# Second matrices of the MLPs: seven products over six input tiles instead of four, and two of the weight sums made by adding transfers

## The chip, the cores and the metric

The kernel runs on one core of one Trainium2 chip. The metric is the device time of one execution in microseconds. Engines are named as in the profile: PE (matmul), PEld (its weight load), DVE (vector), ACT (scalar), POOL (GpSimd), SP (issues the transfers); `SPq` and the like are an engine's sequencer. Tensors in SBUF have 128 partitions; PSUM holds banks of 128 x 512 float32.

## The reference, cut to what matters

An encoder trunk of two layers for 256 rows (`T`) of width 2048 (`D`) in float32. Both layers have an attention and a squared-ReLU MLP; the change is in the MLPs:

```python
def sq_relu_mlp(h, g, w1, w2):
    a = jax.nn.relu(rms_norm(h, g) @ w1)
    return (a * a) @ w2

h = h + sq_relu_mlp(h, mlp_norm_g[layer], mlp_w1[layer], mlp_w2[layer])   # 2048 -> 8192 -> 2048
```

All else (the first layer's attention with a forget gate, shared keys and values, the second layer's attention over chunks with a position bias, the output projections) is computed by both kernels in the same way.

## The kernel before, in words

**Products.** Activations are stationary, weights stream: a matmul takes a 128 x 128 block of the transposed activations and 512 columns of a weight tile. For float32 accuracy every operand is split into a high part that PE's fp32r form holds exactly and a low rest, and each product is three passes (`passes`, L408, L410, L412): high by high, low activation by high weight, high activation by low weight. A **unit** is 128 x 1024 of weights: two input tiles (of the 16 that make up 2048) by one **panel** of 512 output columns. With two blocks of 128 rows it has 2 x 2 x 3 = 12 matmuls.

**Feeding.** `units` lists all weights in the order of use. `load` (L164) has SP bring a unit to one of four `raw` buffers; `issue` (L175) has ACT write its high part (L184) and DVE the low one (L185) to three buffers each (`hi`, `lo`); `fetch` (L188) keeps three split units and three loaded ones ahead of PE. `keep_order` (L35) ties the instructions of DVE, ACT, PE and SP to the order in which the program writes them, so each engine works in that order and an instruction that waits holds up what stands behind it.

**Fill.** Side work (attention steps, turning an output through DRAM so that it is the next product's activations, squaring) lies in slots: `run_fill` runs one slot after each unit, `add_fill` appends. A step that has to wait for PE, a transfer or another engine is thus put some units later.

**The MLP.** `mlp` (L769) goes through four chunks of 2048 hidden columns. A chunk has two pairs of panels of the first matrix and two **pairs** of the second one, which adds the chunk's hidden tiles to the output. In each pair, 4 of the 16 input tiles, two rows blocks and the two panels form a 2 x 2 by 2 x 2 block product; with half the input tiles, one row block and one panel per entry it would take eight products. The kernel takes the seven of Strassen's scheme in Winograd's form: "11" and "22" and "21" are weight blocks as they are, T1, T2, T3, T4 are sums of them. Each product is a **form** (`Form`), with two input tiles: 1 x 2 x 3 = 6 matmuls (`form_products`). The sums on the side of the activations (`sums`, L230) are made once per chunk or layer.

`Pair.items` names the work: `f0` to `f6` are the forms in the order 11, T3, T2, T1, 21, T4, 22; `a2` to `a7` and `b2` to `b7` the units of the other 12 input tiles for the two panels. The order of a pair is `f0 rest f1 rest f2 rest f3`, where `rest` is the previous pair's `b5 b6 b7`, and then the string in `head`. Four PSUM banks hold the pair, and forms land in more than one entry: f1's product is copied out by ACT to `P7` (L856), f0's bank copied (L853), and DVE adds the pieces to other banks after f2 (L837) and after `a2` (L845).

**The tiles of a pair.** `prepare` (L762) runs after each unit. `Pair.units` says at how many units before the pair's f0 the tiles 12, 11, 22, 21 are brought (`bring`, L744, transfers by SP to buffers named `k` and `v`, two of each, which the attention uses at other times), and T1 and T3 are made (`make`, L747, a DVE add or subtract at L760). T1 and T3 go to buffers named `bias`, of which there are two, shared with the attention's bias and the scaled input `y` in `split_turned`; the first pair uses the attention's `prob` room. T2 is made over 12 after f0 and T4 over 11 after f1.

**POOL** does a few small things in the attention (an inverse root per head, a mask) and none in the MLP.

Of the kernel before, what the change touches and what calls it, by code (L numbers as in the profile page):

```python
# [15 lines left out]
P = 128  # L16
T = 256
# [14 lines left out]
REL = 384  # L32

# [13 lines left out]
def trunk(ctx: ExitStack, tc: tile.TileContext, xT, xr, gs, hg, bf, wgate, w_in, w_oa, w1a, w2a,  # L47
          w_kv, w_qb, w_ob, w1b, w2b, rel, out):
# [23 lines left out]
    def load_x(i):  # L72
        raw_x[i] = qkv.tile([P, GH, T], F32, name="xin", tag="kv"[i // 2], bufs=2)
        SY.dma_start(raw_x[i], xT[:, i * GH : (i + 1) * GH, :])
# [9 lines left out]
    ones = const.tile([P, T], F32, name="ones")  # L84
    V.memset(ones, 1.0)
    warm = ps_o.tile([P, 512], F32, name="pt", tag="po")
    for _ in range(11):
        TE.matmul(warm[:, :P], ones[:, :P], ones[:, :P], start=True, stop=True)
# [18 lines left out]
    class Form:  # L107

        def __init__(self, pair, i):
            self.pair, self.name = pair, ("11", "T3", "T2", "T1", "21", "T4", "22")[i]  # L110
# [8 lines left out]
    class Pair:  # L119
# [3 lines left out]
        def __init__(self, src, first, order, third):  # L123
            self.src = [[src[first + q * 8 + u] for u in range(8)] for q in range(2)]
            self.third, self.ps, self.t, self.room, self.units = third, None, {}, None, (9, 8, 7, 6, 5, 2)
            self.head = {"early": "a2 f4 a3 f5 b2 f6 b3 a4 b4 a5 a6 a7", "late": "a2 f4 a3 f5 b2 f6 b3 a4 a5 b4 a6 a7",
                         "": "a2 f4 a3 f5 a4 f6 a5 a6 a7 b2 b3 b4"}[order]

        def items(self, names):
            return [(self, "abf".index(i[0]), int(i[1])) for i in names.split()]  # L130

    def plan_mlp(w1, w2, tail):
        n, pairs = w1.shape[0] // NCH, []
        for c in range(NCH):
            for src, late in ((w1, ""), (w2, "late")):
                for q in range(2):
                    pairs.append(Pair(src, c * n + 16 * q, (late if pairs else "early") if q == 0 else "", len(pairs) % 2 == 0))
        pairs[0].units, pairs[1].units, pairs[2].units = (15, 13, 11, 8, 10, 8), (9, 8, 7, 6, 3, 2), (9, 8, 7, 6, 1, 2)
# [6 lines left out]
        units.extend(Form(p, i) if q == 2 else p.src[q][i] for p, q, i in plan)  # L145
        return plan
# [6 lines left out]
    plan_a = plan_mlp(w1a, w2a, tail_a)  # L153
# [5 lines left out]
    plan_b = plan_mlp(w1b, w2b, tail_b)  # L159
# [15 lines left out]
    def issue(parts=1):  # L175
        if not raws:
            load(parts)
        raw, cuts = raws.popleft()
        if not cuts:
            raw, cuts = raw.pair.t[raw.name], [slice(0, UN)]  # L180
        hi = wsp.tile([P, UN], F32R, name="hi")
        lo = wsp.tile([P, UN], F32R, name="lo")
# [3 lines left out]
        ready.append((hi, lo))  # L186

    def fetch(ahead=AHEAD, early=EARLY):  # L188
        while (units or raws) and len(ready) <= ahead:
# [3 lines left out]
        return ready.popleft()  # L193
# [36 lines left out]
    def sums(a, fs):  # L230

        w = [wk.tile([P, 512], F32, name="sum", tag="wk") for _ in range(2)]

        def part(i):
            v = w[i // 2][:, i % 2 * 256 : i % 2 * 256 + 256].rearrange("p (g t) -> p g t", g=2)
# [739 lines left out]
```

## Time and profile before

| | |
|---|---|
| median of 3 runs | 2108.54 us (2107.03, 2108.95, 2108.54) |
| the profiled execution | 2109.01 us, of which its span is 2107.2 us |
| granted TensorE clock | 1.00 of full speed |
| transfers | 491.63 MB, mean 233 GB/s; queue q1 took 71.2% of 16 engines' time |
| instructions | PE 9332, DVE 1812, ACT 1431, POOL 47 |

A page's first part gives each engine's busy time, its share of the span and its count of instructions. A matmul's length in a row is the time from its start to its modelled end, and matmuls overlap, so the pace is read from starts. In rows of groups, `x638 | 775.8, 1219 | 296.3 <-ACT ...` is: count, busy us and mean ns of one, idle us of the engine just before them and what ended it. In windows, "x" is the count in brackets behind the busy us; then come granted clock, DMA share and GB/s. Rows of transfers have the count, the size and the median us from issue to landing. Lines (L408) are those of the kernel before; in parts on the changed kernel they are its own.

### The profile page before, as it was taken

Reading aid. Unit: us, or ns where it says so; the run is one execution under the profiler, and the core shown is the slowest. Engines: PE = TensorE matmul, PEld = TensorE weight load, DVE = VectorE, ACT = ScalarE, POOL = GpSimd, SP = SyncE. Lnnn points to the kernel's source line nnn. Section 1 sums busy time; section 2 is a strip of 40 time slices with the busy share of each in tenths; the row PEclk is TensorE's granted clock in tenths of the full one; section 3 lists DMA queues with packets and bytes.
Section 4 is the critical chain, followed back from the end, with each engine's and each line's share of the span. In section 5 each row is a group of like instructions: output and inputs, shape, how many; then the busy total and the mean of one; then the engine's idle time right before and its main releaser. Section 6 shows DMA issues by size and latency. Waiting matters only on the chain.

```text
span 2107.2 us, 26036 instructions
## 1 busy us (share of the span) xinstructions
PE 2099.1 (100%) x9332; PEld 1741.2 (83%) x9332; DVE 1587.3 (75%) x1812; ACT 1191.4 (57%) x1431; POOL 48.7 (2%) x47
## 2 busy tenths in 40 slices
PE   9999999999999999999999999999999999999999
PEld 8788888888888888888888888888888888888887
DVE  6777676887788777778767677678877877887775
ACT  6545455665466565556575455456654654665653
POOL 1001000000000000000001000000000000000000
PEclk9999999999999999999999999999999999999999
DMA  8787778776676676577678777787766666766774
GB/s 289 236 257 231 234 250 272 241 238 231 216 241 212 211 250 230 188 245 259 194 242 259 238 233 233 227 279 240 257 227 202 232 230 217 236 216 210 244 239 146
DMA packets 182594, 491.63 MB, mean 233 GB/s; under 512 B 36784, under 2 KB 74048, under 8 KB 182464
## 3 DMA queue, kind: packets, MB, share of 16 engines
q1 hardware_dynamic: 182464, 489.96, 71.2%
q8 instruction: 73, 1.20, 0.2%
q14 instruction: 57, 0.47, 0.1%
HBM read 450.01 MB, written 39.87 MB: 232 GB/s over the span
## 4 chain that ended last, share of the span: by engine, by line
PE 99%; DMA 1%; SPq 0%; ACT 0%; DVE 0%; issue 0%; DVEq 0%; ACTq 0%
PE acc L408 26%; PE acc L410 26%; PE acc L412 26%; PE s L408 6%; PE s L412 6%; PE s L410 6%; DMA raw<-in_w_in 1%; PE po L581 1%; PE s L550 1%; PE po L582 0%; PE s L549 0%; PE s L670 0%; DMA turn<-z 0%; SPq L294 0%; ACT hi L184 0%
## 5 line engine op out<-in xcount | busy, mean ns | idle before, releaser
L185 DVE TENSOR_TENSOR lo<-raw,hi 128x1024 fp32r<-128x1024 f32 (+1 forms) x642 | 778.3, 1216 | 296.8 <-ACT hi L184 286.5
L184 ACT ACTIVATE hi<-raw 128x1024 fp32r<-128x1024 f32 (+1 forms) x642 | 677.6, 1057 | 515.2 <-PE acc L410 394.7
L408 PE MATMUL acc<-hi,act 128*128 128x512 f32 x2306 | 632.9, 393 | 2.9 <-ACT hi L184 2.9
L410 PE MATMUL acc<-hi,act 128*128 128x512 f32 x2306 | 623.8, 389 | 0.0
L412 PE MATMUL acc<-lo,act 128*128 128x512 f32 x2306 | 623.5, 389 | 0.0
L410 PEld LDWEIGHTS acc<-hi,act 128*128 128x128 f32 x2306 | 432.8, 188 | 90.4
L412 PEld LDWEIGHTS acc<-lo,act 128*128 128x128 f32 x2306 | 432.8, 188 | 89.9
L408 PEld LDWEIGHTS acc<-hi,act 128*128 128x128 f32 x2306 | 430.8, 188 | 90.9 <-ACT hi L184 3.8
L184 ACT ACTIVATE hi<-w 128x1024 fp32r<-128x1024 f32 x160 | 169.5, 1059 | 153.8 <-PE acc L410 94.4
L185 DVE TENSOR_TENSOR lo<-w,hi 128x1024 fp32r<-128x1024 f32 x160 | 194.8, 1218 | 69.3 <-ACT hi L184 68.3
L408 PE MATMUL s<-hi,act 128*128 128x512 f32 x448 | 121.1, 389 | 0.0
L410 PE MATMUL s<-hi,act 128*128 128x512 f32 x448 | 121.0, 389 | 0.0
L412 PE MATMUL s<-lo,act 128*128 128x512 f32 x448 | 121.0, 389 | 0.0
L184 ACT ACTIVATE hi<-wT 128x1024 fp32r<-128x1024 f32 x60 | 63.6, 1059 | 62.1 <-PE acc L410 41.6
L410 PEld LDWEIGHTS s<-hi,act 128*128 128x128 f32 x448 | 84.1, 188 | 17.5
L412 PEld LDWEIGHTS s<-lo,act 128*128 128x128 f32 x448 | 84.1, 188 | 17.5
L408 PEld LDWEIGHTS s<-hi,act 128*128 128x128 f32 x448 | 84.0, 188 | 17.4
L185 DVE TENSOR_TENSOR lo<-wT,hi 128x1024 fp32r<-128x1024 f32 x60 | 73.2, 1220 | 28.0 <-ACT hi L184 27.8
L760 DVE TENSOR_TENSOR wT<-w,w 128x1024 f32<-128x1024 f32 x60 | 73.1, 1218 | 0.0
L584 ACT ACTIVATE act<-po 128x256 fp32r<-128x256 f32 x32 | 12.3, 385 | 91.1 <-PE po L582 91.1
L492 POOL TENSOR_TENSOR rn<-vv,mhalf 128x4 f32<-128x4 f32 x32 | 43.3, 1366 | 389.9 <-DVE vv L491 389.7
L585 DVE TENSOR_TENSOR act<-po,act 128x256 fp32r<-128x256 f32 x32 | 13.6, 425 | 51.3 <-ACT act L584 51.3
(164 smaller groups left out, 1347.7 us busy)
## 6 DMA issues: line engine op xcount, KB each, us to landing
raw<-in_w_in SPq DMA_DIRECT2D x96, 512.0 KB, 4.5
raw<-in_w1a SPq DMA_DIRECT2D x96, 512.0 KB, 4.3
raw<-in_w2a SPq DMA_DIRECT2D x96, 512.0 KB, 4.4
raw<-in_w1b SPq DMA_DIRECT2D x96, 512.0 KB, 4.3
raw<-in_w2b SPq DMA_DIRECT2D x96, 512.0 KB, 4.3
raw<-in_w_kv SPq DMA_DIRECT2D x64, 512.0 KB, 4.5
turn<-z SPq DMA_DIRECT2D x60, 512.0 KB, 4.2
q<-turn SPq DMA_DIRECT2D x168, 128.0 KB, 3.9
```

What stands on the lines that cost most here:

```text
L184: S.activation(hi[:, c], raw[:, c], AF.Copy)
L185: V.tensor_tensor(lo[:, c], raw[:, c], hi[:, c].bitcast(F32), op=ALU.subtract)
L408: TE.matmul(ps[:, cols], xh, cut(hi, j), start=first, stop=False, **kw)
L410: TE.matmul(ps[:, cols], xl, cut(hi, j), start=False, stop=False, **kw)
L412: TE.matmul(ps[:, cols], xh, cut(lo, j), start=False, stop=last, **kw)
L492: G.tensor_tensor(rn, vv, mhalf, op=ALU.pow)
L550: TE.matmul(s[:, P : 3 * P], q[:, a, P:T], k[:, a], start=True, stop=True)
L581: TE.matmul(po[:, :T], v[:, 0, a * P : (a + 1) * P], pT[:, :2], start=True, stop=False)
L584: S.activation(o[i][:, 0], po[:, :T], AF.Copy)
L585: V.tensor_tensor(o[i][:, 1], po[:, :T], o[i][:, 0].bitcast(F32), op=ALU.subtract)
L760: V.tensor_tensor(t[name], t[a], t[b], op=op)
```

## The change

For the second matrices (`w2`), the seven products now take six input tiles instead of four. Such pairs are called **wide**: a weight block has 128 x 1536 (`WIDE`), and the host lays `w2` out in two arrays, blocks of 1536 columns for the products (`w2f`) and units for the other ten input tiles (`w2s`). Each form consists of `f`, two input tiles and 6 matmuls as before, and a half `h`, the third tile with 128 x 512 and 3 matmuls, which has one split buffer each (`hih`, `loh`). The order in a wide pair is `f0 h0 rest f1 h1 rest f2 h2 rest f3 h3 a3 f4 h4 b3 f5 h5 a4 f6 h6 b4 a5 a6 a7`; the first matrices' pairs keep four input tiles and the order of before.

All signs are turned so that every weight sum is an addition. T2 goes over T3, T1 over 12, T4 over 11 (first matrices) or over T2 (wide). In wide pairs T1 and T4 are transfers that POOL issues (`put`, L801) and that add a block from HBM to what lies in SBUF; T2 is summed as soon as T3 is split and T4 added as soon as T2 is split. f0 and f1 have changed banks: after f1 ACT copies its bank to `P7` (L873) and writes minus f0's bank into it (L874), on which f2 goes on; DVE's first sum has turned signs.

The sums of hidden tiles are made for the third tile too. The units at which tiles are brought and summed, and the slots of the hidden tiles' steps, have other numbers. `bias` has one buffer of 1536 columns instead of two, and small tiles of the first attention lie in it at the start. The core of the diff:

```diff
+WIDE = UN + 512
...
+        def plan(self, rest):
+            made = [self.items(f"f{i} h{i}" if self.wide else f"f{i}") for i in range(7)]
+            own = {"early": "a2 F a3 F b2 F b3 a4 b4 a5 a6 a7", "": "a2 F a3 F a4 F a5 a6 a7 b2 b3 b4",
+                   "wide": "a3 F b3 F a4 F b4 a5 a6 a7"}[self.order].split()
+            plan = made[0] + rest[:1] + made[1] + rest[1:2] + made[2] + rest[2:] + made[3]
+            n = 4
+            for i in own:
+                if i == "F":
+                    plan += made[n]
+                    n += 1
+                else:
+                    plan += self.items(i)
+            return plan, self.items("b5 b6 b7")
...
+            for q in range(2):
+                at = c * n + 16 * q
+                src = [[w1[at + 8 * j + u] for u in range(8)] for j in range(2)]
+                order = "" if pairs else "early"
+                when = (25, 20, 9, 15, 10, 8) if not pairs else (9, 7, 8, 6, 3, 2) if q and not c else (9, 7, 8, 6, 5, 1) if q else (7, 5, 6, 4, 3, 2)
+                pairs.append(Pair({k: src[int(k[1]) - 1][int(k[0]) - 1] for k in names}, src, order, len(pairs) % 2 == 0, when))
+            for q in range(2):
+                at = 2 * c + q
+                src = [[None] * 3 + [w2s[10 * at + 5 * j + u] for u in range(5)] for j in range(2)]
+                when = (7, 5, 6, 4, 3, 2) if q else (9, 7, 8, 6, 5 if c else 3, 1)
+                pairs.append(Pair({k: w2f[4 * at + i] for i, k in enumerate(names)}, src, "wide", len(pairs) % 2 == 0, when))
         plan, rest = [], [(tail, 0, u) for u in range(KT // UA - 3, KT // UA)]
         for p in pairs:
-            f = p.items("f0 f1 f2 f3")
-            plan += [f[0], rest[0], f[1], rest[1], f[2], rest[2], f[3]] + p.items(p.head)
-            rest = p.items("b5 b6 b7")
...
+            form, half = raw, raw.half
+            raw, cuts = form.pair.t[form.name], [slice(0, 512 if half else UN)]
+            if half:
+                raw = raw[:, UN:]
+        n = cuts[-1].stop
+        hi = wsp.tile([P, n], F32R, name="hi" if n == UN else "hih", bufs=3 if n == UN else 1)
+        lo = wsp.tile([P, n], F32R, name="lo" if n == UN else "loh", bufs=3 if n == UN else 1)
         for c in cuts:
             S.activation(hi[:, c], raw[:, c], AF.Copy)
             V.tensor_tensor(lo[:, c], raw[:, c], hi[:, c].bitcast(F32), op=ALU.subtract)
-        ready.append((hi, lo))
+        ready.append((hi, lo, n < UN))
+        if form and half == form.pair.wide:
+            if form.name == "T3":
+                make(form.pair, "T2")
+            elif form.name == "T2" and half:
+                put(form.pair, "T4")
+
+    def half_next():
+        u = raws[0][0] if raws else units[0]
+        return isinstance(u, Form) and u.half
...
-        while (units or raws) and len(ready) <= ahead:
+        while (units or raws) and sum(1 for r in ready if not r[2]) <= ahead and not (half_next() and any(r[2] for r in ready)):
...
-        V.tensor_tensor(part(0), a[1][0], a[1][1], op=ALU.add)
-        V.tensor_tensor(part(1), part(0), a[0][0], op=ALU.subtract)
-        V.tensor_tensor(part(2), a[0][0], a[1][0], op=ALU.subtract)
+        V.tensor_tensor(part(0), a[1][0], a[1][1], op=ALU.subtract)
+        V.tensor_tensor(part(1), a[0][0], part(0), op=ALU.subtract)
+        V.tensor_tensor(part(2), a[1][0], a[0][0], op=ALU.subtract)
         V.tensor_tensor(part(3), a[0][1], part(1), op=ALU.subtract)
...
+    def room(tag, name, dtype=F32):
+        return qkv.tile([P, WIDE], dtype, name=name, tag=tag, bufs=1 if tag == "bias" else 2)
...
+                c = {3: 0, 2: 1, 1: 2, 6: 3}[i]
+                c = c * P if half else c * 256 + g * P
+                xp = [fs[k + 2 * half][:, c : c + P] for k in range(2)]
+            items.append((ps[i not in (4, 5)][i in (0, 5)], xp, g % 2, i < 2 and g == 0, i < 2 and g == stop))
...
     def bring(p, name):
-        t = qkv.tile([P, UN], F32, name="w" + name, tag="kv"[name[1] == "2"], bufs=2)
-        SY.dma_start(t, p.src[int(name[1]) - 1][int(name[0]) - 1])
-        p.t[name] = t
+        p.t[name] = room("kv"[name in ("12", "21")], "w" + name)
+        SY.dma_start(p.t[name][:, : WIDE if p.wide else UN], p.big[name])
 
     def make(p, name):
         t = p.t
-        if name in ("T1", "T3"):
-            if p.room is not None:
-                t[name] = p.room[:, (name == "T3") * UN : (name == "T3") * UN + UN]
-            else:
-                t[name] = qkv.tile([P, GH * REL], F32, name="w" + name, tag="bias", bufs=2)[:, :UN]
-        elif name == "T2":
-            t[name] = t["12"]
+        if name == "T3":
+            t[name] = prob.tile([P, 9 * 3 * P], F32, name="wT3", tag="p", bufs=1) if p.order == "early" else room("bias", "wT3")
         else:
-            t[name] = t["11"]
-        a, b, op = {"T1": ("12", "11", ALU.subtract), "T3": ("22", "12", ALU.subtract),
-                    "T2": ("T3", "11", ALU.add), "T4": ("21", "T2", ALU.subtract)}[name]
-        V.tensor_tensor(t[name], t[a], t[b], op=op)
+            t[name] = t[{"T1": "12", "T2": "T3", "T4": "11"}[name]]
+        a, b = {"T1": ("12", "11"), "T3": ("22", "12"), "T2": ("T3", "11"), "T4": ("21", "T2")}[name]
+        d, a, b = (t[i][:, : WIDE if p.wide else UN] for i in (name, a, b))
+        V.tensor_tensor(d, a, b, op=ALU.add)
+
+    def put(p, name):
+
+        at, other = {"T1": ("12", "11"), "T4": ("T2", "21")}[name]
+        p.t[name] = p.t[at]
+        G.dma_start(p.t[name][:, :WIDE], p.big[other], accum_op=ALU.add)
 
     def prepare(p, d):
-        if d == p.units[0] and p.units[0] > 9:
-            p.room = prob.tile([P, 9 * 3 * P], F32, name="wTT", tag="p", bufs=1)
-        for name, at in zip(("12", "11", "22", "21", "T1", "T3"), p.units):
+        for name, at in zip(("12", "22", "21", "11", "T3", "T1"), p.units):
             if d == at:
-                (make if name[0] == "T" else bring)(p, name)
+                (bring if name[0] != "T" else put if p.wide and name == "T1" else make)(p, name)
...
+            f, kind, k = plan[i - 1]
+            done = k if i and kind > 1 and kind == 2 + f.wide else None
+            if done == 1:
+                f.t["P7"] = wk.tile([P, 512], F32, name="p7", tag="wk")
+                S.activation(f.t["P7"], f.ps[1][0], AF.Copy)
+                S.activation(f.ps[1][0], f.ps[1][1], AF.Copy, scale=-1.0)
+            if q > 1:
+                form_products(p.ps, hi, lo, p.x, p.fs, u, q == 3, 1 + p.wide)
+                if u == 2 and q == 2 + p.wide:
+                    V.scalar_tensor_tensor(p.ps[0][1], p.ps[1][0], -1.0, p.t["P7"], op0=ALU.mult, op1=ALU.subtract)
             else:
                 products(p.ps[q], hi, lo, p.x, u, not units and not ready, p.fast)
+                if p.fast and (q, u) == (0, p.own):
+                    V.tensor_tensor(p.ps[1][1], p.ps[1][0], p.t["P7"], op=ALU.add)
                 run_fill()
                 if u == KT // UA - 1:
                     for b in range(NB):
                         p.evac[q](b, p.ps[q][b])
-                if p.fast and (q, u) == (0, 2):
-                    V.tensor_tensor(p.ps[1][1], p.ps[1][0], p.t["P7"], op=ALU.add)
                 nxt = next((j for j in starts if j > i), None)
                 if nxt is not None:
                     d = sum(1 for it in plan[i:nxt] if it[1] < 2)
                     prepare(plan[nxt][0], d)
-            if i and plan[i - 1][1:] in ((2, 0), (2, 1)):
-                f = plan[i - 1][0]
-                if plan[i - 1][2] == 0:
-                    S.activation(f.ps[0][0], f.ps[1][0], AF.Copy)
-                else:
-                    f.t["P7"] = wk.tile([P, 512], F32, name="p7", tag="wk")
-                    S.activation(f.t["P7"], f.ps[1][1], AF.Copy)
-                    make(f, "T4")
+            if done == 1 and not f.wide:
+                make(f, "T4")
+            elif done == 2:
+                S.activation(f.ps[0][0], f.ps[1][1], AF.Copy)
```

More of the change, by code (lines that the diff above doesn't have):

```diff
@@ L121, in trunk @@
         fast = True
[L123 to L127, printed above, removed]
-        def items(self, names):
-            return [(self, "abf".index(i[0]), int(i[1])) for i in names.split()]
@@ L132, in plan_mlp, with __init__ @@
-    def plan_mlp(w1, w2, tail):
+        def __init__(self, big, src, order, third, units):
+            self.big, self.src, self.third, self.units, self.order = big, src, third, units, order
+            self.ps, self.t, self.wide, self.own = None, {}, order == "wide", 3 if order == "wide" else 2
+        def items(self, names):
+            return [(self, "abfh".index(i[0]), int(i[1])) for i in names.split()]
+        def plan(self, rest):
[11 more added lines that the diff above has]
+            return plan, self.items("b5 b6 b7")
@@ L133, in plan_mlp @@
+    def plan_mlp(w1, w2f, w2s, tail):
         n, pairs = w1.shape[0] // NCH, []
+        names = ("11", "12", "21", "22")
         for c in range(NCH):
[L135 to L138, printed above, removed]
+            for q in range(2):
[9 more added lines that the diff above has]
+                pairs.append(Pair({k: w2f[4 * at + i] for i, k in enumerate(names)}, src, "wide", len(pairs) % 2 == 0, when))
@@ L433, in products, with form_products @@
                 passes(items, hi, lo, c, **kw)
-    def form_products(ps, hi, lo, x, fs, i):
+    def form_products(ps, hi, lo, x, fs, i, half, stop):
         items = []
-        for g in range(2):
+        for g in (2,) if half else range(2):
             if i in (0, 4, 5):
@@ L647, in head_gains @@
         yield
-    wgr = const.tile([P, KT * H], F32, name="wgr")
+    early = room("bias", "early")
+    wgr = early[:, : KT * H]
     ct = {}
@@ L886, in rel_bias @@
     def rel_bias(g, box):
-        rb = qkv.tile([P, GH, REL], F32, name="bias")
+        rb = room("bias", "rb").rearrange("p (a t) -> p a t", a=GH)
         src = bass.AP(tensor=rel.tensor, offset=rel.offset + g * GH * REL, ap=[[1, P], [REL, GH], [1, T]])
@@ L942 @@
     rel = np.zeros((H, REL), np.float32)
+    wide = [_wide(i["mlp_w2"][j]) for j in range(2)]
     rel[:, REL - i["b_rel"].shape[2] :] = i["b_rel"][0]
```

116 lines of the change are left out of this document (58 added, 58 removed).

## The prediction

> **What bounds the kernel now.** I read the page's engine table first, then its chain, then who PE waited for, and last the time lines of one steady pair.
>
> ```profile
> span 2107.2 us, 26036 instructions
> ...
> PE 2099.1 (100%) x9332; PEld 1741.2 (83%) x9332; DVE 1587.3 (75%) x1812; ACT 1191.4 (57%) x1431; POOL 48.7 (2%) x47
> ...
> PE 99%; DMA 1%; SPq 0%; ACT 0%; DVE 0%; issue 0%; DVEq 0%; ACTq 0%
> ...
> PEld acc L408 <- ACT hi L184: 3.8, 3, 2.0
> ...
> PE acc L408 <- ACT hi L184: 2.9, 2, 1.6
> ```
>
> PE is busy for all but 8.1 us of the span, and the chain that ended last is PE from end to end. PE waits for another engine hardly at all: the two wait rows (total, times, longest) are all that there is of it between its first matmul and its last, 3 and 2 times. So time goes away only with matmuls, and every stall that the change makes on PE counts in full. The profiled execution took 2109.01 us, 1.81 us more than its span; the median of the three runs is 2108.54 us, 0.47 us below the profiled one. I sum in differences and put them on the median.
>
> The price of one matmul comes from PE's time line in a second-matrix pair (columns: start, length, engine, line, what, count). The form f1 has three passes of two matmuls, `rest` three passes of four.
>
> ```profile
> 506.62 0.61 PE L410 MATMUL acc<-hi,Sh 128*128 128x512 f32 x2
> 507.07 0.62 PE L412 MATMUL acc<-lo,Sh 128*128 128x512 f32 x2
> 507.52 1.07 PE L408 MATMUL s<-hi,act 128*128 128x512 f32 x4
> 508.43 1.07 PE L410 MATMUL s<-hi,act 128*128 128x512 f32 x4
> 509.34 1.07 PE L412 MATMUL s<-lo,act 128*128 128x512 f32 x4
> 510.24 0.62 PE L408 MATMUL acc<-hi,Sh 128*128 128x512 f32 x2
> 511.60 1.07 PE L408 MATMUL s<-hi,act 128*128 128x512 f32 x4
> ...
> 502.08:544.24 42.16, 42.16 (x187) 34.92 (x186) 32.40 (x31) 21.15 (x22) 0.00 (x0) 1.00 0.59 199
> 628.56:670.72 42.16, 42.16 (x187) 34.92 (x186) 32.47 (x30) 26.64 (x28) 0.00 (x0) 1.00 0.73 243
> ```
>
> A unit of 12 matmuls takes 510.24 - 507.52 = 2.72 us, a form of 6 takes 511.60 - 510.24 = 1.36 us, so one takes 0.2267 us. Two windows follow, each from one pair's f0 to the next pair's: the second and the first pair of a chunk's second matrix (columns: length, busy PE, PEld, DVE, ACT, POOL with counts, clock, DMA share, GB/s). Both are 42.16 us = 186 x 0.2267, with no gap, at full granted clock. DVE has 9.7 us free, ACT more, and the DMA engines are 59% and 73% busy. That is the room the change must live in.
>
> **What goes.** A second-matrix pair had 7 forms of 6 matmuls and 24 units of which 4 are replaced, so 12 x 12 + 42 = 186. With six input tiles it has 7 forms of 6, 7 halves of 3 and 10 units of 12: 63 + 120 = 183. That is 3 per pair, in 16 pairs (2 layers x 4 chunks x 2): 48 matmuls x 0.2267 = **-10.9 us**. The order of the built program agrees: PE has 48 instructions fewer, nothing else of PE changes in number. The first matrices keep their 186.
>
> **What comes on DVE and ACT.** Durations:
>
> ```profile
> L184 ACT ACTIVATE hi<-raw 128x1024 fp32r<-128x1024 f32 x638 | 675.3, 1060 | 514.9 <-PE acc L410 394.7 <-PE s L410 76.7 <-DMA raw<-in_w_in 14.7
> L184 ACT ACTIVATE hi<-raw 128x512 fp32r<-128x512 f32 x4 | 2.3, 620 | 0.3 <-DMA raw<-in_w_in 0.3
> L185 DVE TENSOR_TENSOR lo<-raw,hi 128x1024 fp32r<-128x1024 f32 x638 | 775.8, 1219 | 296.3 <-ACT hi L184 286.0 <-PE acc L410 4.6 <-DMA q<-turn 2.9
> L185 DVE TENSOR_TENSOR lo<-raw,hi 128x512 fp32r<-128x512 f32 x4 | 2.6, 686 | 0.5 <-ACT hi L184 0.5
> L760 DVE TENSOR_TENSOR w<-w,w 128x1024 f32<-128x1024 f32 x32 | 38.9, 1217 | 0.0
> L853 ACT ACTIVATE acc<-s 128x512 f32<-128x512 f32 x16 | 9.3, 582 | 0.0
> L856 ACT ACTIVATE p<-acc 128x512 f32<-128x512 f32 x16 | 9.3, 582 | 0.0
> ```
>
> DVE per pair before: 19 splits x 1.219 + 4 sums x 1.217 = 28.0 us. After: 17 x 1.219 + 7 half splits x 0.686 + 2 sums over 1536 columns. No row has 1536; going on from 512 to 1024 (0.686 to 1.219) gives 1.75 us, between one and two of the 1.217. Sum 29.0 us: +1.0 us in a pair that is 0.7 us shorter, so about 33.4 of 41.5 us. ACT: 17 x 1.060 + 7 x 0.620 + 3 x 0.582 against 19 x 1.060 + 2 x 0.582, +2.8 us. The new sums of hidden tiles (four short DVE adds and one split per chunk) fall in first-matrix pairs, beside PE. All this I cost at nothing, hidden by PE; the cover ends only where one of them is what PE waits for next. There is one such place.
>
> **The new wait in front of f2.** Before, f1's product went to a bank of its own and f2 went on in f0's bank, with only a copy to be made later. Now f1 and f2 share `ps[1][0]`: after f1 and its half h1, ACT must copy the bank out (P7) and overwrite it with minus M1; f2's first matmul waits for the second. ACT's own time line at that place before:
>
> ```profile
> 507.32 1.06 ACT L184 ACTIVATE hi<-raw 128x1024 fp32r<-128x1024 f32 x1 [0.64 <-PE acc L410]
> 508.28 0.58 ACT L856 ACTIVATE p<-acc 128x512 f32<-128x512 f32 x1
> 509.54 1.07 ACT L184 ACTIVATE hi<-wT 128x1024 fp32r<-128x1024 f32 x1 [0.67 <-PE s L410]
> ...
> 84.08 1.06 ACT hi L184
> 85.15 0.04 issue
> 85.19 1.20 PE acc L408 x4
> ```
>
> Two ACT instructions follow each other 0.10 us closer than their lengths (507.32 to 508.28 for one of 1.06), and PE starts 0.05 us after the ACT result it waits for (85.14 to 85.19). In a first-matrix pair the next split starts 0.2 us before `rest` (507.32 against 507.52), P7 ends 1.34 after its start, the negated copy at about 1.98, and PE needs f2 only at 2.72: hidden, by 0.7 us. In a wide pair the half-split of T2 stands ahead of it, and its single buffer is free only when h1's second pass ends, at about the start of `rest` (t = 0; as before, 0.09 us after a pass that ends 0.39 us from its last start). Then: half split 0.03 to 0.65, split of the next unit 0.55 to 1.61, P7 1.51 to 2.09, negated copy, which overwrites what P7 reads and so can't overlap it, 2.14 to 2.72, PE at 2.77 to 2.81 instead of 2.72. I take **0.1 us x 16 = +1.6 us**. This holds if ACT is free at t = 0. Before it come, from the end of h0's second pass 4.7 us earlier: T3's half on ACT 0.62 and on DVE 0.69, T2's sum 1.75, T2's split on ACT 1.06, together 4.1 and the hand-overs: some 0.5 us to spare. Bounds: 0 below; above, a sum of 2 x 1.217 us and a DVE step of 0.69 in front of it eat the 0.5 and give 0.9 us more.
>
> **The adding transfers.** T1 and T4 of wide pairs are no longer DVE sums but transfers issued by POOL that add the other tile from HBM, 768 KB each, 32 in all. The trace has neither an adding transfer nor one by POOL. The nearest rows:
>
> ```profile
> raw<-in_w2a SPq DMA_DIRECT2D x96, 512.0 KB, 4.4
> w<-in_w2a SPq DMA_DIRECT2D x32, 512.0 KB, 5.3
> bias<-cd SPq DMA_DIRECT2D x4, 768.0 KB, 6.7
> ...
> 73.25 10.75 DMA raw<-in_w_in
> ```
>
> Counted with 2.72, 1.36 and 0.68 us from the end of h1: T4's transfer may start when T2's half is split, at about 1.5. PE is at f3 from 7.5, a3 from 9.5, f4 from 12.2, b3 from 14.3, f5 from 17.0; f5's low pass starts at 17.9, and one ACT split and one DVE split (2.4 us with their hand-overs) come before it. So T4 must land by 15.5: **14.0 us**, and until then nothing but ACT waits. Behind the waiting split on ACT stand h5's and a4's; PE needs a4 only at 19.0, so they are not worse off. T1 starts when T3 is summed and has more (some 17 us). POOL has nothing else there (0.00 busy in both windows), so nobody queues behind it. For the cost I take 10 us, nearest to the 6.7 us row and something for the sum's second operand; the ends are 6.7 and, from the 10.75 us that 512 KB took in the crowded start, 1.5 x 10.75 = 16.1 us. At 10 us it costs PE **nothing**. The Trainium skill's page "Collectives: The Full Stack" (section "The bandwidth ceiling: the fold count and why AG ≠ RS ≠ AR") says that an add in a transfer reads two sources, and that those reads, not the arithmetic, halve the rate. By that, an estimate from the row is 2 x 6.7 = 13.4 us: still in time, with 0.6 us left; no run shown here tests it.
>
> The tiles themselves move the same bytes (4 x 768 KB and 10 x 512 KB for 4 and 12 of 512 KB). The adds bring 1.57 MB per pair. 199 GB/s at a share of 0.59 means 337 GB/s at full share, so one reading of the operands adds 1.57 MB / 337 GB/s = 4.7 us, 0.11 of share: 0.70 and 0.84. If they count twice, 0.82 and 0.95.
>
> **What is moved.** SP issues the four tiles one to three units later or earlier than before, each behind the raw loads already waiting there; 22 is now read by T3 two units after its issue (in a first pair at 7 and 5), that is 5.4 us and a form, 6.8 us, against 5.3 us to landing. DVE that waits there for 1 us has its 9.7 us of slack per pair. The attention's bias, the scaled input and T3 share one buffer instead of two; in program order each starts after the other's last read, and SP would wait for a DVE step of the same unit. I cost this at 0; a place where it isn't so costs about one stall as the longest above, 1.6 us. Tile loads, start and end are else the same.
>
> **Sum:** -10.9 + 1.6 = -9.3; 2109.01 - 9.3 = 2099.7 for a profiled execution, **2099.2 us** on the median.
>
> **Rivals.**
> - *DMA crowding takes half.* In the eight first pairs the share goes to 0.84 or 0.95 while tiles, raw loads and turns are due. For: the 73% and the 5.3 us tiles. Against: three raw loads are ahead, and PE stalls nowhere in these windows now. If three of the eight have a stall as the longest above, 3 x 1.6 = +4.8: 2104.0 us.
> - *f2 waits longer.* In the eight second pairs DVE's queue in front of T2's sum also holds the residual adds of the previous pair:
>
> ```profile
> 501.83 1.41 DVE L528 SCALAR_TENSOR_TENSOR h<-acc,qm,h 128x512 f32<-128x512 f32 x2 [0.86 <-PE acc L412]
> ```
>
>   If they push it past the margin, by the upper bound: 8 x 0.9 = +7.2: 2106.4 us. Against: they start 0.25 us before f0 (502.08) and end 5.6 us before the end of h1 in the new order; with one split of 1.22 behind them, DVE is free 4.4 us before that end, and T3's half reaches it 0.3 us later.
> - *Slower: T4 lands too late.* It decides at 14.0 us; above, PE waits in front of f5 in all 16 pairs. At the 16.1 us end: 16 x 2.1 = 33.6, so 2099.2 + 33.6 = 2132.8 us. The change as a whole is slower from 14.0 + 9.3 / 16 = 14.6 us on. For: the transfer is of a kind that no row shows, in competition with SP's queue. Against: the 6.7 us row and the 10 us taken stay well below.
>
> **How the numbers follow.** Forecast 0.62, crowding 0.15, f2 0.08, T4 late 0.15. Less than 0.2% (4.2 us, about what a measurement of this kernel can tell from no change) is the line: faster is below 2104.3 us. The forecast and half of the crowding case, which lies on the line, are faster, 0.70; the other half and the f2 case are within, 0.15; T4 late is slower, 0.15. The range goes from no f2 wait (2108.5 - 10.9 = 2097.6, less the spread of runs) to above the crowding and f2 cases: 2097.2 to 2107.0. It leaves out the 0.15 of T4 late.
>
> **What would show it.** PE 9284 matmuls. Pair windows of 41.5 us and a little. A PE wait for ACT's negated copy of about 0.1 us, 16 times; none of PE in front of f5. Adds landing in under 14 us; shares of 0.70 to 0.82 and 0.84 to 0.95. ACT waiting for an add without PE behind it would still agree. Wrong would be: PE waits for DMA-fed splits in wide pairs, a matmul interval other than 0.2267 us in the halves (three into one bank in a row), or new stalls outside the second-matrix pairs.

## The result and the profile after

The changed kernel is slower: 2129.41 us (median of 4 runs, 2124.7 to 2136.17) against 2108.51 us (4 runs, 2107.03 to 2108.95), ratio 1.0102, 95% interval 1.0088 to 1.0116. The forecast was 2099.2 us (range 2097.2 to 2107.0), faster. The profiled execution took 2127.72 us; its page, with the lines that answer to those shown of before:

```profile
span 2126.0 us, 26197 instructions
...
PE 2097.6 (99%) x9284; PEld 1733.1 (82%) x9284; DVE 1609.3 (76%) x1900; ACT 1233.3 (58%) x1551; POOL 76.8 (4%) x80
...
PE 86%; DMA 7%; ACT 3%; DVE 2%; issue 1%; SPq 1%; ACTq 0%; DVEq 0%
```

PE does the 48 matmuls less (9284), but is idle for 28.4 us instead of 8.1, and busy for 1.5 us less instead of 10.9. The chain of work that ended last, 99% PE before, now goes through a transfer and ACT for a tenth of the span. The waits (total us, times, longest) name the place:

```profile
ACT q L814 <- DMA q<-turn: 35.2, 14, 4.7
PE s L446 <- ACT s L874: 19.1, 8, 3.2
PE acc L446 <- ACT acc L874: 1.5, 2, 1.1
```

L874 is the negated copy in front of f2. PE waits for it 8 times in banks named `s` and twice in `acc`: the `s` ones are the eight **first** pairs of a chunk's second matrix. The first row is new too: ACT's Relu of a turned hidden tile waits for that tile's columns, 14 times, where before it was 4 times and 1.8 us in all. The two belong together, as ACT's time line at one first pair shows (f0 at 460.29):

```profile
468.38 1.06 ACT L814 ACTIVATE q<-q 128x1024 f32<-128x1024 f32 x1 [2.69 <-DMA q<-turn]
469.35 1.04 ACT L209 ACTIVATE hi<-wT 128x1024 fp32r<-128x1024 f32 x1
470.30 0.61 ACT L209 ACTIVATE hih<-wT 128x512 fp32r<-128x512 f32 x1
470.81 1.04 ACT L209 ACTIVATE hi<-raw 128x1024 fp32r<-128x1024 f32 x1
471.76 0.58 ACT L873 ACTIVATE p<-s 128x512 f32<-128x512 f32 x1
472.37 0.58 ACT L874 ACTIVATE s<-s 128x512 f32<-128x512 f32 x1
```

```profile
467.09 1.07 PE L446 MATMUL acc<-hi,act 128*128 128x512 f32 x4
...
473.00 0.74 PE L446 MATMUL s<-hi,Sh 128*128 128x512 f32 x2 [2.72 <-ACT s L874]
```

Read it from below. PE starts f2 as the negated copy ends (472.95). That copy stands in ACT's order behind P7, a split of an ordinary unit, the split of T2 (its half last), and the Relu. The Relu waited 2.69 us; in the eight first pairs it waited 1.95 to 4.70 us, 27.8 of the 35.2 us in all. T2's sum, which the split needs, was there earlier, on DVE:

```profile
466.12 1.76 DVE L795 TENSOR_TENSOR wT<-wT,w 128x1536 f32<-128x1536 f32 x1
```

It ended at 467.88, so T2's split could have begun 1.47 us earlier than it did (469.35); that is a good half of this pair's stall of 2.72 us. In five of the eight first pairs T2's sum was done earlier than its split by more than the whole stall. Why were the columns late? The turn has two steps: SP writes the tile to DRAM (`turn<-z`), waits until the write has landed, and then issues the four reads that bring the columns back (`q<-turn`). SP's and POOL's time lines at the pair shown:

```profile
459.34 2.40 SPq L332 DMA_DIRECT2D q<-turn  x4
```

```profile
458.29 1.05 POOL L801 DMA_DIRECT2D w<-in_w2fa  x1 [185.55 <-DMA raw<-in_w1a]
```

Here, in the first chunk of a layer, T1's adding transfer, 768 KB, starts a microsecond ahead of the four reads. They land 7.2 us (median) after their issue, against 2.8 us before (the changed kernel, then before):

```profile
q<-turn SPq DMA_DIRECT2D x4, 128.0 KB, 7.2
```

```profile
q<-turn SPq DMA_DIRECT2D x4, 128.0 KB, 2.8
```

The second layer's first chunk is alike (1.9 us ahead). In the other six first pairs it is not the reads but the write ahead of them that is late. The same place one chunk later, POOL and SP of the changed kernel and then SP of before:

```profile
623.94 0.85 POOL L801 DMA_DIRECT2D w<-in_w2fa  x1 [107.67 <-DVE wT L795]
```

```profile
625.79 0.33 SPq L326 DMA_DIRECT2D turn<-z  x1
634.82 1.75 SPq L332 DMA_DIRECT2D q<-turn  x4
```

```profile
621.56 0.33 SPq L288 DMA_DIRECT2D turn<-z  x1
626.41 1.75 SPq L294 DMA_DIRECT2D q<-turn  x4
```

T1's transfer starts 1.9 us ahead of the write, the write lands after 9.0 us instead of 4.8 (8.2 to 9.7 in the six pairs, 3.9 to 5.7 before), and the reads, issued only then, take no longer than before. In that chunk before, ACT ran the Relu 2.1 us after f0 (628.56) without a wait:

```profile
630.68 1.05 ACT L775 ACTIVATE q<-q 128x1024 f32<-128x1024 f32 x1
```

### The profile page after: what moved, and what is told of

Same layout as the page of the kernel before. It is cut to its first block, busy times and chain, and to the rows that moved or that the text cites. A ratio compares the mean times of both kernels' runs of the same rounds, so it can differ in the third digit from the quotient of the medians.

```text
span 2126.0 us, 26197 instructions
## 1 busy us (share of the span) xinstructions
PE 2097.6 (99%) x9284; PEld 1733.1 (82%) x9284; DVE 1609.3 (76%) x1900; ACT 1233.3 (58%) x1551; POOL 76.8 (4%) x80
## 4 chain that ended last, share of the span: by engine, by line
PE 86%; DMA 7%; ACT 3%; DVE 2%; issue 1%; SPq 1%; ACTq 0%; DVEq 0%
PE acc L446 23%; PE acc L448 22%; PE acc L450 22%; PE s L446 6%; PE s L450 5%; PE s L448 5%; DMA turn<-z 3%; DMA q<-turn 2%; ACT hi L209 2%; DVE lo L210 1%; DMA raw<-in_w1a 1%; SPq L332 1%; DMA raw<-in_w_in 1%; PE po L620 1%; PE s L589 1%
## 5 line engine op out<-in xcount | busy, mean ns | idle before, releaser
L210 DVE TENSOR_TENSOR lo<-raw,hi 128x1024 fp32r<-128x1024 f32 (+1 forms) x610 | 739.1, 1216 | 264.9 <-ACT hi L209 259.1
L209 ACT ACTIVATE hi<-raw 128x1024 fp32r<-128x1024 f32 (+1 forms) x610 | 640.8, 1053 | 360.6 <-PE acc L448 269.0
L446 PE MATMUL acc<-hi,act 128*128 128x512 f32 x2210 | 608.6, 394 | 2.3 <-ACT hi L209 2.3
L448 PE MATMUL acc<-hi,act 128*128 128x512 f32 x2210 | 598.7, 389 | 0.0
L450 PE MATMUL acc<-lo,act 128*128 128x512 f32 x2210 | 598.5, 389 | 0.0
L448 PEld LDWEIGHTS acc<-hi,act 128*128 128x128 f32 x2210 | 415.1, 188 | 87.0 <-DVE act L297 0.2
L446 PEld LDWEIGHTS acc<-hi,act 128*128 128x128 f32 x2210 | 413.8, 188 | 87.3 <-ACT hi L209 3.3
L210 DVE TENSOR_TENSOR lo<-w,hi 128x1024 fp32r<-128x1024 f32 x144 | 175.3, 1218 | 75.8 <-ACT hi L209 74.6
L209 ACT ACTIVATE hi<-wT 128x1024 fp32r<-128x1024 f32 x80 | 84.6, 1058 | 69.0 <-DVE wT L795 25.6
L210 DVE TENSOR_TENSOR lo<-wT,hi 128x1024 fp32r<-128x1024 f32 x80 | 97.6, 1221 | 27.8 <-ACT hi L209 26.6
L209 ACT ACTIVATE hih<-w 128x512 fp32r<-128x512 f32 x64 | 40.2, 628 | 61.4 <-PE acc L448 49.6
L210 DVE TENSOR_TENSOR loh<-w,hih 128x512 fp32r<-128x512 f32 x64 | 44.1, 688 | 19.4 <-ACT hih L209 18.3
```

Source lines behind the costliest of these rows:

```text
L209: S.activation(hi[:, c], raw[:, c], AF.Copy)
L210: V.tensor_tensor(lo[:, c], raw[:, c], hi[:, c].bitcast(F32), op=ALU.subtract)
L446: TE.matmul(ps[:, cols], xh, cut(hi, j), start=first, stop=False, **kw)
L448: TE.matmul(ps[:, cols], xl, cut(hi, j), start=False, stop=False, **kw)
L450: TE.matmul(ps[:, cols], xh, cut(lo, j), start=False, stop=last, **kw)
```

## The experiments

**Theory:** two places in ACT's own order make f2 late: the Relu step, waiting for the columns, stands ahead of T2's split, and the two copies of f1's bank stand behind the next unit's split. **Rivals:** the adding transfers' traffic as such; DVE, on which T2's sum of 1536 columns comes too late. (The letters in the expectations mean what each spells out beside them; B and C are not the same in all of them.) Every kernel was compared with the kernel before on the same chip; before was 2107.5 to 2107.8 us there.

**The Relu step one unit later** (label relu_later):

```diff
-uses = ((4, 5, 7, 8, 9, 10), (4, 5, 6, 7, 8, 9), (4, 5, 6, 8), (3, 4, 4, 4))[n]
+uses = ((4, 5, 7, 8, 9, 10), (4, 5, 6, 7, 8, 9), (5, 6, 6, 7), (3, 4, 4, 4))[n]
```

> The third hidden quarter's steps (relu, two squares, low part) move from slots 3, 4, 5, 7 to 4, 5, 5, 6, so relu stands behind the negated copy on ACT instead of in front of T2's split. Theory A (the stall in front of f2 is ACT standing still on the turned columns, with T2's split, two more splits, P7 and the negated copy queued behind): the stalls of 1.8 to 3.2 us in the eight first pairs and the low clock behind two of them go; counted over the time line they are 25 us with restart and clock, so 2129.4 - 25 = 2104 us, between 2101 and 2107. Theory B (the five ACT steps are too long by themselves): the first pairs keep 1 us or more, time 2118 or above.

The four numbers place the Relu, two squares and the low part of that tile; the first square goes one unit later too, and the low part one earlier.

2110.57 us, 1.0011 (1.0002 to 1.002): some 19 of the 21 us go with these four numbers. It is above the 2101 to 2107 us of theory A, so something is left, and far below the 2118 of B. Its waits:

```profile
ACT hi L209 <- DVE wT L795: 57.9, 25, 3.6
ACT q L814 <- DMA q<-turn: 5.7, 9, 1.9
PE s L446 <- ACT s L874: 4.4, 4, 1.4
PE acc L446 <- ACT acc L874: 3.9, 5, 1.4
```

The columns hardly matter any more (5.7 us), though they are no earlier: the write still takes 8.6 to 10.3 us in the six pairs. PE's wait in first pairs falls from 19.1 to 4.4 us. What ACT waits for now is T2's sum on DVE: behind the first cause stands a second, smaller one, the DVE rival's.

**The copies ahead of the next split** (label copy_first):

```diff
 for i, (p, q, u) in enumerate(plan):
-    hi, lo = fetch()
-    if p.ps is None:
-        open_pair(p)
     f, kind, k = plan[i - 1]
...
         S.activation(f.ps[1][0], f.ps[1][1], AF.Copy, scale=-1.0)
+    hi, lo = fetch()
+    if p.ps is None:
+        open_pair(p)
```

> P7 and the negated copy are written ahead of the two splits that stood before them (T2's half, 0.62 us, and the next unit, 1.06 us). Theory A: relu still waits for the columns, but the chain behind it is 1.5 us shorter, so stalls of 1.8 to 3.2 us become 0.3 to 1.7 us, and the second pairs' 0.1 to 1.3 us go: 8 x 1.5 + 3 = 15 us and some clock less, 2110 to 2116 us. Theory B: the chain alone is the cause and fits once it is 1.5 us shorter: all goes, 2102 us or less.

2115.28 us, 1.0047 (1.0028 to 1.0065), as the theory expected. The negated copy is L871 here:

```profile
PE s L446 <- ACT s L871: 9.9, 8, 2.4
```

The waits of the second pairs are gone, those of the first are halved; the columns still hold up ACT (42.7 us, 16 times). A small new one appears in the first pairs: DVE's sum in front of f3, 0.2 to 0.3 us each time.

**T1 back on DVE** (label t1_on_dve), and **T1 and T4 on DVE** (label sums_on_dve):

```diff
-(bring if name[0] != "T" else put if p.wide and name == "T1" else make)(p, name)
+(bring if name[0] != "T" else make)(p, name)
```

For the second also `make(form.pair, "T4")` in place of `put`, with T2's tile as its target.

> T1 of wide pairs is a DVE sum of 1536 columns (1.75 us) again; T4 stays an adding transfer. Theory C (T1's adding transfer, which starts 1 us ahead of the column transfers, is what makes these take 7.2 instead of 2.8 us): relu no longer waits, the first pairs' stalls go, 2102 to 2110 us. Theory D (the crowding comes from the 768 KB tiles and raw loads that stand before the columns in SP's own queue): columns still land late, at most 1 us per first pair is won, 2118 to 2132 us.

> Both T1 and T4 of wide pairs are DVE sums; six input tiles and all else as in the changed kernel. It tells what the adding transfers are worth. DVE gets 2 x 1.75 us more per wide pair, some 37 of 41.5 us. Theory C: close to the run with T1 alone on DVE, 2100 to 2110 us. Theory D: as the changed kernel or worse, 2120 to 2140 us, with PE waiting for DVE's low parts as well.

2132.31 us, 1.0117 (1.0101 to 1.0134), and 2137.98 us, 1.0145 (1.0127 to 1.0162). The waits of the first:

```profile
ACT hi L209 <- DVE wT L795: 64.5, 23, 4.4
PE s L446 <- ACT s L874: 10.4, 8, 1.4
PE acc L446 <- ACT acc L874: 8.5, 8, 1.4
ACT q L814 <- DMA q<-turn: 7.6, 7, 2.5
```

Both times miss what theory C forecast (2102 to 2110 and 2100 to 2110 us). Yet C's cause holds: without T1's transfer the columns come in time (7.6 us instead of 35.2), and the write takes 4.5 to 5.6 us in the six pairs, so it is that transfer which delays them. No time is won, because the 1.75 us that DVE does instead come ahead of T2's sum (in the pair shown above it starts at 467.25 instead of 466.12), and now all 16 pairs have a stall of up to 1.4 us. The second run has theory D's time without D's cause: there too ACT waits only 12.9 us for the columns. Whether the transfers cost time once ACT's order is mended, these two runs don't tell; the next two, which keep the transfers, do.

**Both orders together** (label both_orders), the two edits above in one kernel, and **also T2's sum in two parts** (label both_orders_t2_in_two):

```diff
-        V.tensor_tensor(d, a, b, op=ALU.add)
+        for c in (slice(0, UN), slice(UN, WIDE)) if p.wide and name == "T2" else (slice(None),):
+            V.tensor_tensor(d[:, c], a[:, c], b[:, c], op=ALU.add)
```

> The hidden tile's Relu step one unit later and ACT's two copies of f1's bank ahead of the next unit's split, together. Theory A (two places in ACT's own order make f2 late): what each edit left is taken by the other. The Relu step later left PE waits of up to 1.4 us for the negated copy; the copies ahead of the split come some 1.06 us earlier, so 0 to 0.4 us are left, and DVE's sum in front of f3 adds 0.25 us in eight pairs. 2101 to 2105 us; PE's waits for ACT's copy under 3 us in all. Theory C (DVE is what makes f2 late: T2's sum of 1536 columns comes too late for ACT): as with the Relu step later alone, 2109 to 2112 us, PE's waits for the copy about as there (8 us in all). Theory B (the adding transfers' traffic itself): no better than the Relu step later alone either, with DMA-fed waits of ACT that stay.

> As both orders together, and T2's sum on DVE in two instructions, of 1024 and 512 columns, so that ACT can split the first part without the second: 0.5 us earlier, for 0.15 us more DVE time per wide pair (estimate from 1.22 and 0.69 against 1.75 us). Theory A: T2's split is no longer last after both orders are mended, so no difference beyond 2 us: 2100 to 2105 us. Theory C: up to 0.5 us in 16 pairs, 8 us less than both orders together.

2104.11 us, 0.9984 (0.9975 to 0.9992), and 2101.72 us, 0.9975 (0.9965 to 0.9985): both faster than the kernel before, 25 and 28 us faster than the change as it was. For the first the theory's time held, and PE no longer waits for ACT's copies anywhere. The second is within the theory's range, 2.4 us below the first (at most 2 were expected), with intervals that overlap; its waits of PE, complete:

```profile
PE acc L446 <- ACT hi L209: 1.2, 3, 0.6
PE pt L89 <- DVE mhalf L91: 1.1, 1, 1.1
PE acc L450 <- DVE lo L210: 0.2, 1, 0.2
```

and ACT and PE at the same first pair, where f2 starts right behind the unit before it (three passes of 0.90, 1.30 and 1.05 us to the next start, a 0.23 us wait among them, not a stall of 2.72):

```profile
465.62 1.06 ACT L209 ACTIVATE hi<-wT 128x1024 fp32r<-128x1024 f32 x1 [1.64 <-DVE wT L796]
466.58 0.58 ACT L871 ACTIVATE p<-s 128x512 f32<-128x512 f32 x1
467.19 0.58 ACT L872 ACTIVATE s<-s 128x512 f32<-128x512 f32 x1
467.69 0.62 ACT L209 ACTIVATE hih<-wT 128x512 fp32r<-128x512 f32 x1
```

```profile
465.09 1.07 PE L446 MATMUL acc<-hi,act 128*128 128x512 f32 x4
465.99 1.07 PE L448 MATMUL acc<-hi,act 128*128 128x512 f32 x4
467.29 1.21 PE L450 MATMUL acc<-lo,act 128*128 128x512 f32 x4 [0.23 <-DVE lo L210]
468.34 0.62 PE L446 MATMUL s<-hi,Sh 128*128 128x512 f32 x2
```

**The T2 split alone with the copies first**, the Relu where it was (label copy_first_t2_in_two):

> The changed kernel with the copies ahead of the split and T2 in two parts, but the Relu step where it was. Theory A (the Relu step stands ahead of T2's split on ACT and waits for the turned columns): T2 in two can't help where ACT waits for the columns; the eight first pairs keep stalls of 1 to 2 us and the time is that of the copies alone less 0 to 3 us: 2112 to 2116 us. Theory C (DVE's T2 is what is late): most of the 8 us go, 2103 to 2107 us.

2118.8 us, 1.005 (1.0035 to 1.0065), no better than the copies first alone (3.5 us more, with intervals that overlap, and outside both ranges, on the theory's side): while ACT stands at the Relu, an earlier T2 is worth nothing. That rules DVE out as the first cause.

**The same transfers without the addition** (label plain_transfers). T1 and T4 then hold only the second operand:

```diff
-        G.dma_start(p.t[name][:, :WIDE], p.big[other], accum_op=ALU.add)
+        G.dma_start(p.t[name][:, :WIDE], p.big[other])
```

> T1 and T4 of the wide pairs come by the same POOL transfers, at the same places, but plain: the addition to what the tile holds is left out. One reading of 768 KB less in each of 32. Theory B (the adding transfer's second reading crowds the columns out): ACT's wait for the turned columns falls from 35.2 us to under 10, the transfers land in 5 to 6.5 us instead of 7.6 to 9.4, and the time falls to 2105 to 2113 us. Theory A (the Relu step's place in ACT's order; the columns are late because the transfer is there at all, a microsecond ahead of them): the transfers are some faster, ACT's wait for the columns stays at 20 to 35 us and the time at 2118 to 2128 us.

2119.21 us, 1.0051 (1.0035 to 1.0066). Its queues and POOL transfers, and then those of the changed kernel (queue: packets, MB, share of 16 engines; issues: KB each, median us to landing):

```profile
q0 software_dynamic: 4608, 25.17, 3.6%
...
w<-in_w2fa POOLq DMA_DIRECT2D x8, 768.0 KB, 6.2
wT<-in_w2fa POOLq DMA_DIRECT2D x8, 768.0 KB, 4.5
```

```profile
q0 software_dynamic: 4608, 25.17, 6.8%
...
w<-in_w2fa POOLq DMA_DIRECT2D x8, 768.0 KB, 9.4
wT<-in_w2fa POOLq DMA_DIRECT2D x8, 768.0 KB, 7.6
```

The addition nearly doubles the DMA engines' time for the same bytes (6.8 / 3.6 = 1.9, at the same span) and costs some 3 us of landing time. But ACT waits for the columns as long as before:

```profile
ACT q L814 <- DMA q<-turn: 34.0, 16, 5.2
```

The write in the six pairs takes 7.7 to 8.5 us here, hardly less than with the addition (8.2 to 9.7). So in the traced executions it is a transfer at this place that holds the columns up, and its second reading adds little. That the time falls by 10 us all the same is not explained: the profiled execution, 2127.74 us, is the longest of the four (the others 2117.85 to 2119.61), so its trace does not show where they won, and a larger part of the second reading in those is not excluded.

**What the adding transfers are worth once the orders are mended:** the kernel with both orders and T2 in two parts, with T1 on DVE (label mended_t1_on_dve) and with both sums on DVE (label mended_sums_on_dve), by the edits shown above.

> The kernel with both orders mended and T2 in two parts, with T1 of the wide pairs summed on DVE again and only T4 an adding transfer. DVE gets one sum of 1.75 us per wide pair more. If DVE's queue ahead of T2 now has room for it (the Relu step's copies and the split are no longer late): same within 2 us, 2100 to 2104 us, no PE wait over 0.5 us. If DVE is still as tight as in the changed kernel, where this same edit left a stall of 1.1 to 1.4 us in all 16 pairs: half of those come back, 8 to 12 us: 2110 to 2114 us.

> The same kernel with both sums, T1 and T4, on DVE: no adding transfer at all, DVE 3.5 us per wide pair more. If the adding transfers only take DVE time that is to spare, 2100 to 2105 us. If they are what makes the narrow form possible: DVE is 33.4 + 3.5 us of 41.5 busy, T2 comes late again, PE waits for ACT's copy or T2's split by 1 us in 16 pairs: 2112 to 2122 us, behind the kernel before.

2114.6 us, 1.0035 (1.0022 to 1.0048), and 2132.31 us, 1.0117 (1.0097 to 1.0138): 13 and 31 us more than with the transfers. This is just above what was expected of a tight DVE for the first (2110 to 2114), and worse than expected for the second (2112 to 2122). Nor do the stalls come where they were expected, at ACT's copy or T2's split. The largest of the second run:

```profile
PE acc L450 <- DVE loh L210: 5.7, 7, 1.1
PE acc L446 <- DVE acc L879: 5.2, 7, 1.8
```

PE waits for DVE's low parts and sums at several places, though DVE is busy only 78% of the span (76% with the transfers). In the kernel as changed the same two edits had cost 8.6 us; that it was so little because PE stood at f2 anyway is a reading, not shown.

**The hidden tile's sums one unit earlier**, with the Relu later (label relu_later_sums_earlier) and in the mended kernel (label mended_sums_earlier). The first line moves the sums and their low half; the second, for a layer's first chunk, also the tile's low half, and the sums by two units:

```diff
-(4, 5, 6, 7, 8, 9), (5, 6, 6, 7)
+(4, 5, 6, 7, 7, 8), (5, 6, 6, 7)
...
-uses = (4, 5, 6, 8, 9, 9) if n else (4, 4, 5, 6, 7, 8)
+uses = (4, 5, 6, 7, 7, 8) if n else (4, 4, 5, 6, 7, 8)
```

> The Relu step later, and also the last three steps of the first pair's second hidden tile (its low half, its four short sums with their split on ACT, the sums' low half) one unit earlier, so that none of them falls behind f0 of a wide first pair. What is left after the Relu step later alone are PE waits of 4.4 us in 4 first pairs (s banks) and of 3.9 us in 5 second pairs (acc banks). If those of the first pairs come from the sums' split, which ACT takes ahead of T3's (a wait of 4.71 us for DVE at that place): the 4.4 us fall to under 1.5, those of the second pairs stay, and with the slower passes behind each stall 4 us go: 2105.5 to 2108 us. If T2's sum is late by itself: both stay, 2109 to 2112 us.

> The kernel with both orders mended and T2 in two parts, with the same three steps of the hidden tile one unit earlier. No f2 waits there any more, so nothing to win beyond the 1.2 us that PE still waits for splits: 2100 to 2103 us. Against it: in the narrow pairs, where the steps land now, the sums stand in front of splits, and if PE comes to wait for those, 2104 to 2108 us.

2107.21 us, 1.0 (0.9991 to 1.001), and 2104.24 us, 0.9983 (0.9974 to 0.9992). The first as expected in time, not in its waits. The longest wait in first pairs falls from 1.4 to 0.4 us, but the sum, 3.0 us in 8, was expected under 1.5; those of the second pairs, expected to stay (3.9 us in 5), fall to one:

```profile
PE s L446 <- ACT s L874: 3.0, 8, 0.4
...
PE acc L446 <- ACT acc L874: 1.4, 1, 1.4
```

So part of what was left there came from these sums, which fell behind f0. In the mended kernel it gains nothing (2100 to 2103 us were expected); whether it loses, the overlapping intervals (against 0.9965 to 0.9985) do not tell.

## Why the prediction was wrong, step by step

- **What bounds the kernel, and what goes:** right. PE bounds it, the count fell by 48, the halves run at the usual pace. (Of the "24 units" only 16 stand in a pair; the 12 x 12 + 42 behind it is right.) The mended kernel, that with both orders and T2 in two parts, has span 2099.9 us, 7.3 less than before, of the 10.9. In it PE waits 2.5 us in all; the missing 3.6 us are small breaks, most of 0.1 to 0.5 us, between passes in the MLPs (4.4 us, less 0.8 of idle time that PE has fewer), not followed further.
- **"This holds if ACT is free at t = 0": the step that failed.** The chain of that sum held only steps of the form itself (T3's half, T2's sum, T2's split). ACT's queue also held a fill step, the Relu, which the fill puts into that unit, with a wait for a transfer in front of it. That wait came from the second step that failed, "it costs PE nothing": T1's transfer was given a deadline of its own, but not the transfers beside it a price. In the example ACT comes to T2's half split 3.2 us after t = 0 (470.30 against 467.09). The wait of f2, taken as 1.6 us with 0.9 us more per pair as its upper bound, was 19.1 + 1.5 = 20.6 us of idle PE, nearly all in the eight first pairs; the rival that it waits longer was priced for the second pairs, and for DVE's residual adds. Of the second pairs two had 1.06 and 0.44 us; in the rest f2 came 0.29 us late once and 0.04 us five times, about the 0.1 taken.
- **PE busy:** with the stalls PE's busy time is 2097.6 us, without them, in the mended kernel, 2092.6. Of these 5.0 us, two stretches of lower clock (below) make 2 x 6 x 0.2267 = 2.7; the rest wasn't followed, slower first passes behind the stalls are part of it (0.58 us to the next start in the example, for 0.45). Before, busy time was 2099.1, and 10.9 less would be 2088.2, so 4.4 us of small breaks are left in the mended kernel too. Together -10.9 + 20.6 + 5.0 + 4.4, and 0.3 us less idle elsewhere, is the 18.8 us by which the span grew.
- **"Hidden by PE", the new sums "fall in first-matrix pairs, beside PE":** partly wrong. Their last steps fell behind f0 of a wide pair and took part of the 0.5 us to spare; moving them took the longest stall left there from 1.4 to 0.4 us.
- **The adding transfers:** their own size was right (medians of 7.6 to 9.4 us for the 10 taken, deadline 14.0), no PE wait in front of f5, and so the slower rival, T4 too late, did not happen. That the change came out slower, as this rival had it, is by another mechanism. The operands count nearly twice. The Trainium skill's page "Collectives: The Full Stack" (section "The bandwidth ceiling: the fold count and why AG ≠ RS ≠ AR") gives that reading of two sources as the reason for half the rate in collectives; the 1.9 above agrees for the engines' time, while the landing grew only 1.5 to 1.7 times.
- **"Crowding takes half":** the rival that came nearest, and priced too low. DMA share was 0.90 and 0.71 in a first and a second pair (forecast 0.84 to 0.95 and 0.70 to 0.82). It named the turns beside tiles and raw loads, and it was a turn that came late: its 512 KB write in six first pairs, its four 128 KB reads in two. The stalls came in all eight instead of three, 1.8 to 3.2 us each instead of 1.6. They cost that only because of what stands behind the Relu on ACT: in the mended kernel the write still takes 8.3 to 10.4 us in the six pairs and ACT waits 10.1 us for columns, and PE does not wait for its copies at all.

## What to carry to other kernels

Where a change puts a new step on an engine and PE waits for it, list everything in that engine's order ahead of it, side work from other stages included, and ask of each what it waits for itself: a transfer that comes 4 us late matters not by its size but by what is queued behind the instruction that waits for it. Before giving up a change with fewer matmuls that came out slower, look whether its loss stands at one place in an order that can be moved; here two moves and a split sum turned +1.0% into -0.25%. Ask of a new transfer not only when it must land itself, but what else is in flight beside it and who waits for that. And judge a part (the adding transfers) in the kernel without that stall: beside it they seemed worth 9 us, without it 31.

## What was not expected of the hardware

Two of the eight stalls in front of f2 were followed by a lower granted clock of PE. Windows of 4 us from the first matmul behind three stalls (length, busy PE, PEld, DVE, ACT, POOL with counts, granted clock, DMA share, GB/s):

```profile
1525.34:1529.34 4.00, 4.00 (x11) 3.19 (x12) 2.12 (x3) 2.79 (x4) 0.65 (x1) 0.61 0.67 114
2037.97:2042.00 4.03, 4.03 (x11) 3.17 (x12) 1.69 (x3) 2.29 (x3) 0.41 (x1) 0.58 0.71 117
985.09:989.09 4.00, 4.00 (x17) 3.30 (x18) 2.50 (x4) 3.68 (x5) 0.41 (x1) 1.00 0.72 121
```

The stalls were 2.00, 2.51 and 3.23 us; behind the longest the clock stayed at 1.00, as behind the other five, behind the two shorter ones it was about 0.6 over four microseconds, with 6 matmuls less done in each. The Trainium skill's page "TensorE: Matmul & The Clock Gate" (section "🔬 Part 1: The HAM clock gate (the "warmup" mystery)") explains that by a window of about 3.4 us that runs freely, so that it would depend on where a stall falls in it; the three rows don't contradict that, but no row here shows the window. That page of the Trainium skill wants one idle window for the lower clock, though, and here single stalls of 2.00 and 2.51 us, shorter than that, came before it; the measurement decides.
